# Loading each block of rows in sixteen groups of eight: which row goes to which partition, and what it does to the DMA engines

## The chip, the cores and the metric

The kernel runs on one core of a Trainium2 chip. The metric is the time of one execution in microseconds (us) of device time. Other words used here: PE is the matrix engine, PEld its weight loads, DVE the vector engine, ACT the scalar engine, POOL is GpSimd, SP the engine that issues the loads. Sixteen DMA engines move data from the memory (HBM) into SBUF, which has 128 partitions. A *load* is one DMA instruction; a *packet* is what one DMA engine moves at a time, here one row of a load (five loads of 128 rows of 16 KB left 640 packets of 16,384 bytes in the trace). A load *lands* when all sixteen engines have reported their share by a semaphore update (31 x 16 = 496 of these for the 31 loads of the kernel before). Engines are *in step* when they work on the same rows of their shares at the same time; a *lead* is how far one is ahead of another. *Partners* are two engines of which the author supposed that they hinder each other.

## The reference

For an array of 1024 x 8192 floats, the skewness of each row:

```python
def reference(x):
    mean = np.mean(x, axis=-1, keepdims=True)
    std = np.std(x, axis=-1, keepdims=True)
    z = (x - mean) / (std + 1e-8)
    return np.mean(z ** 3, axis=-1).astype(np.float32)
```

The 33.55 MB of input are read once. All the work is in reading them and in summing x, x squared and x cubed by row.

## The kernel before

Eight blocks of 128 rows, a row per partition. A block comes in 2 to 9 loads of some columns each; `UNITS` lists the widths. ACT squares with a running sum, DVE multiplies the square by x with a running sum, PE adds up transposed 128 x 128 pieces for the sum of x. The results stand as one column per block, are transposed at the end and stored.

```python
UNITS = [
    [512, 1024, 2560, 4096],
    [4096, 4096],
    # ... five blocks cut ...
    [1152, 1152, 1152, 1152, 1024, 896, 896, 512, 256],
]
X_BUFS = 8
# ...
    xv = x.rearrange("(b p) c -> b p c", p=P)
    ob = out.rearrange("(b p) -> b p", p=P)
# ...
    for b, widths in enumerate(UNITS):
        # ...
        for k, w in enumerate(widths):
            xt = xpool.tile([P, w], FP, tag="x", name=f"x_{b}_{k}")
            nc.sync.dma_start(out=xt, in_=xv[b, :, c0 : c0 + w])
            # ... squares on ACT, cubes on DVE, transposes on PE ...
# ...
    skT_ps = psum1.tile([NB, P], FP, tag="skT")
    nc.tensor.matmul(out=skT_ps, lhsT=skew, rhs=ident, start=True, stop=True, is_transpose=True)
```

Of the kernel before, what the change touches and what calls it, by code (L numbers as in the profile page):

```python
# [8 lines left out]
FP = mybir.dt.float32  # L9
# [21 lines left out]
def _slices(w):  # L31
    n = -(-w // SUB_MAX)
    step = -(-w // n // 128) * 128
    return [(s, min(s + step, w)) for s in range(0, w, step)]
# [3 lines left out]
def kernel(  # L38
# [5 lines left out]
    nc = tc.nc  # L44
    P = nc.NUM_PARTITIONS
# [5 lines left out]
    third = (1.0 / 3.0) ** 0.5  # L51
    assert len(UNITS) == NB and all(sum(u) == C for u in UNITS)

    xv = x.rearrange("(b p) c -> b p c", p=P)
    ob = out.rearrange("(b p) -> b p", p=P)


# [6 lines left out]
    onep = ctx.enter_context(tc.tile_pool(name="onep", bufs=1))  # L64
# [7 lines left out]
    nc.scalar.activation(out=tiny, in_=onesn, func=AF.Square)  # L72
    ident = onep.tile([P, P], FP, tag="ident")
    make_identity(nc, ident)
    s2u = onep.tile([P, L * MAXC], FP, tag="s2u")
    s3u = onep.tile([P, L * MAXC], FP, tag="s3u")
    nc.vector.memset(s2u, 0.0)
# [7 lines left out]
    skew = onep.tile([P, NB], FP, tag="skew")  # L85
# [4 lines left out]
    def small(name, n):  # L90
        return onep.tile([P, n], FP, tag=name, name=name)

    def finish_first_blocks():

        m2, m3 = small("m2a", L), small("m3a", L)
        for dst, src in ((m2, s2u), (m3, s3u)):
            nc.vector.tensor_reduce(  # L97
                out=dst, in_=src.rearrange("p (b c) -> p b c", c=MAXC), axis=X_AXIS, op=ALU.add
            )
        m1sq, m1sq3, nm1 = small("m1sqa", L), small("m1sq3a", L), small("nm1a", L)  # L100
        nc.scalar.activation(out=m1sq, in_=s1ps[:, 0:L], func=AF.Square)
        nc.scalar.activation(out=m1sq3, in_=s1ps[:, 0:L], func=AF.Square, scale=third)
        nc.scalar.activation(out=nm1, in_=s1ps[:, 0:L], func=AF.Copy, scale=-3.0)
        g = nc.gpsimd
        var, rr = small("vara", L), small("rra", L)
        g.tensor_tensor(out=var, in0=m2, in1=m1sq, op=ALU.subtract)  # L106
        g.tensor_tensor(out=m1sq3, in0=m1sq3, in1=var, op=ALU.add)  # L107
        g.tensor_tensor(out=m1sq3, in0=m1sq3, in1=nm1, op=ALU.mult)  # L108
        g.tensor_tensor(out=m3, in0=m3, in1=m1sq3, op=ALU.add)  # L109
        g.tensor_tensor(out=rr, in0=var, in1=expo, op=ALU.pow)  # L110
        g.tensor_tensor(out=skew[:, 0:L], in0=m3, in1=rr, op=ALU.mult)  # L111

    def close_block(b, tp):
        tsb = Tsb[b % 2]
        nc.scalar.copy(out=tsb, in_=tp)  # L115
        nc.tensor.matmul(out=s1ps[:, b : b + 1], lhsT=tsb, rhs=onesn, start=True, stop=True)  # L116

    for b, widths in enumerate(UNITS):
        last = b == L
        tp = psum.tile([P, P], FP, tag="tp", name=f"tp_{b}")  # L120
        c0 = 0
        j = 0
        for k, w in enumerate(widths):
            xt = xpool.tile([P, w], FP, tag="x", name=f"x_{b}_{k}")
            nc.sync.dma_start(out=xt, in_=xv[b, :, c0 : c0 + w])
            c0 += w
            for s, e in _slices(w):
                i = b * MAXC + j
                a2 = s2l[:, j : j + 1] if last else s2u[:, i : i + 1]
                a3 = s3l[:, j : j + 1] if last else s3u[:, i : i + 1]  # L130
                j += 1
                in_psum = last and k >= len(widths) - PSUM_SQ
                pool = psq if in_psum else sqpool
                sq = pool.tile([P, e - s], FP, tag="sq", name=f"sq_{b}_{k}_{s}")
                nc.scalar.activation(  # L135
                    out=sq, in_=xt[:, s:e], func=AF.Square, scale=s_scale, accum_out=a2
                )
                cube = cubes[:, 0 : e - s] if in_psum else sq
                nc.vector.scalar_tensor_tensor(  # L139
                    out=cube, in0=sq, scalar=1.0, in1=xt[:, s:e],  # L140
                    op0=ALU.mult, op1=ALU.mult, accum_out=a3,
                )
            n = w // P
            for c in range(n):
                nc.tensor.matmul(  # L145
                    out=tp, lhsT=xt[:, c * P : (c + 1) * P], rhs=ident,
                    start=(k == 0 and c == 0), stop=(c0 == C and c == n - 1),
                    is_transpose=True,
                )
        close_block(b, tp)  # L150
        if b == L - 1:
            finish_first_blocks()
# [14 lines left out]
        out=m3, in0=v3, scalar1=nm1, scalar2=m3, op0=ALU.mult, op1=ALU.add  # L167
# [1 line left out]
    nc.vector.tensor_tensor(out=skew[:, L:NB], in0=m3, in1=rr, op=ALU.mult)  # L169

    skT_ps = psum1.tile([NB, P], FP, tag="skT")
    nc.tensor.matmul(out=skT_ps, lhsT=skew, rhs=ident, start=True, stop=True, is_transpose=True)  # L172
    skT = small("skT", P)[0:NB, :]
    nc.vector.tensor_copy(out=skT, in_=skT_ps)  # L174
    nc.sync.dma_start(out=ob, in_=skT)
# [30 lines left out]
```

## Time and profile before

| | before |
|---|---|
| median time | 92.75 us in the 3 runs known when predicting; 92.5 us with the fourth |
| profiled span | 91.4 us |
| busy: DVE, ACT, PE | 73.9, 69.1, 68.0 us |
| DMA engines, 5 to 80 us | always busy (share 1.00 to 1.01), 413 to 430 GB/s |
| a packet of 16,384 bytes | 611 ns, at the 10th, 50th and 90th percentile |
| first packet, last landing of a load | 1.75 us, 84.9 us |

The lines are shown and read in the prediction. The packet times are computed from the trace's DMA records, which hold start, duration and size of each packet, though not the engine that moved it.

### The profile page before, as it was taken

What the parts mean: (1) busy time and instruction counts of PE and PEld (TensorE: products, weight loads), DVE (VectorE), ACT (ScalarE), POOL (GpSimd) and SP (SyncE); (2) the same over time, 40 slices, a digit from 0 to 9 for tenths busy, and PEclk for the clock granted to TensorE, in tenths of its full rate; (3) what the DMA queues carried; (4) which work ended last, traced back from release to release, by engine and by line L of the source; (5) the groups of instructions that cost most, each with busy time, mean ns of one, the idle gap of its engine ahead of it and who ended that gap; (6) DMA issues with size and microseconds to landing.
All of it is one profiled execution on the core that took longest, in us unless ns stands there. A gap on an engine that the chain in (4) does not pass through costs nothing. (4 is left out here: it accounts for less than half of the span.)

```text
span 91.4 us, 1437 instructions
## 1 busy us (share of the span) xinstructions
PE 68.0 (74%) x529; PEld 60.6 (66%) x529; DVE 73.9 (81%) x91; ACT 69.1 (76%) x101; POOL 9.4 (10%) x14
## 2 busy tenths in 40 slices
PE   0391898879495949688889897857789798989610
PEld 0360897779494939587879796747678687867500
DVE  0052290898989798978999999998899999999960
ACT  6350927969595959689889999766798899999830
POOL 3000000000000000000000000000000000699820
PEclk9999999999999999999999999999999999999995
DMA  1999999999999999999999999999999999991000
GB/s 43 362 374 440 445 438 409 430 452 430 402 423 452 442 417 434 435 424 399 430 414 404 430 420 420 423 407 422 419 409 423 406 418 408 406 344 74 0 0 2
DMA packets 4486, 33.64 MB, mean 368 GB/s; under 512 B 504, under 2 KB 640, under 8 KB 2560
## 3 DMA queue, kind: packets, MB, share of 16 engines
q1 hardware_dynamic: 4480, 33.56, 88.6%
q8 instruction: 4, 0.07, 0.3%
q14 instruction: 2, 0.02, 0.0%
HBM read 33.55 MB, written 0.00 MB: 367 GB/s over the span
## 5 line engine op out<-in xcount | busy, mean ns | idle before, releaser
L139 DVE SCALAR_TENSOR_TENSOR sq<-sq,x 128x2048 f32<-128x2048 f32 (+11 forms) x39 | 71.5, 1885 | 13.9 <-ACT sq L135 13.9
L145 PE MATMUL tp<-ident,x 128*128 128x128 f32 x512 | 65.2, 285 | 15.3 <-DMA x<-in_x_dram 15.0
L135 ACT ACTIVATE sq<-x 128x2048 f32<-128x2048 f32 (+12 forms) x41 | 62.8, 1534 | 17.4 <-DMA x<-in_x_dram 15.9
L145 PEld LDWEIGHTS tp<-ident,x 128*128 128x128 f32 x512 | 58.7, 147 | 20.5 <-DMA x<-in_x_dram 16.6
L106 POOL TENSOR_TENSOR vara<-m2a,m1sqa 128x7 f32<-128x7 f32 x1 | 1.3, 1294 | 77.1 <-DVE m3a L97 77.1
L135 ACT ACTIVATION_READ_ACCUMULATOR sq<-x 128x1 f32 x41 | 7.6, 186 | 0.0
L116 PEld LDWEIGHTS s1ps<-onesn,tsb 128*128 128x128 f32 x16 | 2.4, 188 | 5.6 <-ACT tsb L115 5.6
L116 PE MATMUL s1ps<-onesn,tsb 128*128 128x1 f32 x16 | 3.1, 260 | 3.7 <-ACT tsb L115 3.7
L139 DVE DVE_READ_ACCUMULATOR sq<-sq,x 128x1 f32 x39 | 3.2, 83 | 0.0
L110 POOL TENSOR_TENSOR rra<-vara,expo 128x7 f32<-128x7 f32 x1 | 2.6, 2624 | 0.0
L115 ACT COPY tsb<-tp 128x128 f32<-128x128 f32 x8 | 2.0, 249 | 0.0
L72 ACT ACT_TABLE_LOAD x1 | 1.3, 1283 | 0.7 <-PEq L190 0.7
L172 PE MATMUL skT_ps<-ident,skew 128*8 128x128 f32 x1 | 0.3, 273 | 2.0 <-DVE skew L169 2.0
L172 PEld LDWEIGHTS skT_ps<-ident,skew 128*8 128x8 f32 x1 | 0.1, 83 | 2.1 <-DVE skew L169 2.1
L107 POOL TENSOR_TENSOR m1sq3a<-m1sq3a,vara 128x7 f32<-128x7 f32 x1 | 1.2, 1202 | 0.1
L139 DVE SCALAR_TENSOR_TENSOR cubes<-sq,x 128x512 f32<-128x512 f32 (+1 forms) x2 | 1.1, 554 | 0.1
L108 POOL TENSOR_TENSOR m1sq3a<-m1sq3a,nm1a 128x7 f32<-128x7 f32 x1 | 1.1, 1150 | 0.0
L109 POOL TENSOR_TENSOR m3a<-m3a,m1sq3a 128x7 f32<-128x7 f32 x1 | 0.9, 935 | 0.1
L111 POOL TENSOR_TENSOR skew<-m3a,rra 128x7 f32<-128x7 f32 x1 | 0.9, 933 | 0.1
L70 DVE MEMSET onesn<- 128x1 f32 x1 | 0.1, 59 | 0.8 <-PEq L190 0.8
L163 POOL TENSOR_TENSOR rrl<-varl,expo 128x1 f32<-128x1 f32 x1 | 0.6, 562 | 0.6 <-ACT varl L161 0.6
L174 DVE COPY skT<-skT_ps 8x128 f32<-8x128 f32 x1 | 0.3, 278 | 0.4 <-PE skT_ps L172 0.4
(25 smaller groups left out, 4.4 us busy)
## 6 DMA issues: line engine op xcount, KB each, us to landing
x<-in_x_dram SPq DMA_DIRECT2D x5, 2048.0 KB, 18.7
x<-in_x_dram SPq DMA_DIRECT2D x5, 1024.0 KB, 24.2
x<-in_x_dram SPq DMA_DIRECT2D x4, 576.0 KB, 9.8
x<-in_x_dram SPq DMA_DIRECT2D x1, 2176.0 KB, 33.8
x<-in_x_dram SPq DMA_DIRECT2D x1, 1920.0 KB, 36.2
x<-in_x_dram SPq DMA_DIRECT2D x2, 896.0 KB, 15.8
x<-in_x_dram SPq DMA_DIRECT2D x1, 1664.0 KB, 33.9
x<-in_x_dram SPq DMA_DIRECT2D x1, 1408.0 KB, 30.3
```

The source lines that it names most:

```text
L72: nc.scalar.activation(out=tiny, in_=onesn, func=AF.Square)
L106: g.tensor_tensor(out=var, in0=m2, in1=m1sq, op=ALU.subtract)
L107: g.tensor_tensor(out=m1sq3, in0=m1sq3, in1=var, op=ALU.add)
L108: g.tensor_tensor(out=m1sq3, in0=m1sq3, in1=nm1, op=ALU.mult)
L109: g.tensor_tensor(out=m3, in0=m3, in1=m1sq3, op=ALU.add)
L110: g.tensor_tensor(out=rr, in0=var, in1=expo, op=ALU.pow)
L111: g.tensor_tensor(out=skew[:, 0:L], in0=m3, in1=rr, op=ALU.mult)
L115: nc.scalar.copy(out=tsb, in_=tp)
L116: nc.tensor.matmul(out=s1ps[:, b : b + 1], lhsT=tsb, rhs=onesn, start=True, stop=True)
L135: nc.scalar.activation(out=sq, in_=xt[:, s:e], func=AF.Square, scale=s_scale, accum_out=a2)
L139: nc.vector.scalar_tensor_tensor(out=cube, in0=sq, scalar=1.0, in1=xt[:, s:e], op0=ALU.mult, op1=ALU.mult, accum_out=a3,)
L145: nc.tensor.matmul(out=tp, lhsT=xt[:, c * P : (c + 1) * P], rhs=ident, start=(k == 0 and c == 0), stop=(c0 == C and c == n - 1), is_transp ...
```

## The change

The comment that came with it: "Within a block partition 8e+i takes row 16i+e, so that the sixteen DMA engines read neighbouring rows; the last transpose puts them back". The hope is a better reading order in the memory.

```diff
-    xv = x.rearrange("(b p) c -> b p c", p=P)
+    xv = x.rearrange("(b i e) c -> b e i c", e=16, i=8)
@@
+    unperm = onep.tile([P, P], FP, tag="unperm")
+    nc.gpsimd.tensor_copy(
+        out=unperm.rearrange("p (i e) -> p i e", e=16),
+        in_=ident.rearrange("p (e i) -> p i e", e=16),
+    )
@@
-            nc.sync.dma_start(out=xt, in_=xv[b, :, c0 : c0 + w])
+            nc.sync.dma_start(out=xt, in_=xv[b, :, :, c0 : c0 + w])
@@
-    nc.tensor.matmul(out=skT_ps, lhsT=skew, rhs=ident, start=True, stop=True, is_transpose=True)
+    nc.tensor.matmul(out=skT_ps, lhsT=skew, rhs=unperm, start=True, stop=True, is_transpose=True)
```

## The prediction

The forecast came to 92.75 + 75 x 0.5 = 130 us, from a worst case of 92.75 + 75 = 168 us. What is measured in it is the 92.75 us, the 75 us of full stream and the 611 ns; that a packet takes twice as long when partners are in step, and that half a load apart costs nothing, was supposition. Rival (c) is that partners hinder each other (theory P of the experiments).

> **What bounds the kernel now.** I read the busy shares first, then the strips over time, then the groups with their idle time, then the waits of the compute engines and of the load queue, and last the end of the run.
>
> ```profile
> PE 68.0 (74%) x529; PEld 60.6 (66%) x529; DVE 73.9 (81%) x91; ACT 69.1 (76%) x101; POOL 9.4 (10%) x14
> ...
> DVE  0052290898989798978999999998899999999960
> ...
> DMA  1999999999999999999999999999999999991000
> GB/s 43 362 374 440 445 438 409 430 452 430 402 423 452 442 417 434 435 424 399 430 414 404 430 420 420 423 407 422 419 409 423 406 418 408 406 344 74 0 0 2
> DMA packets 4486, 33.64 MB, mean 368 GB/s; under 512 B 504, under 2 KB 640, under 8 KB 2560
> ...
> q1 hardware_dynamic: 4480, 33.56, 88.6%
> ```
>
> No compute engine is full over the span of 91.4 us, but the DMA strip is: from the second slice (2.3 us each) to the thirty-sixth it stands at 9, and the rate is 400 to 450 GB/s throughout. So the sixteen DMA engines are the first suspect. The windows give the same in numbers:
>
> ```profile
> 5.00:20.00 15.00, 11.46 (x70) 10.34 (x71) 8.05 (x11) 8.62 (x12) 0.00 (x0) 1.00 1.01 426
> 20.00:40.00 20.00, 15.57 (x134) 14.46 (x133) 18.30 (x17) 15.86 (x19) 0.00 (x0) 1.00 1.01 430
> 40.00:60.00 20.00, 17.79 (x154) 16.52 (x153) 19.21 (x21) 18.55 (x23) 0.00 (x0) 1.00 1.00 419
> 60.00:80.00 20.00, 16.23 (x133) 14.10 (x132) 19.09 (x23) 16.88 (x26) 1.53 (x2) 1.00 1.01 413
> ```
>
> The columns are the stretch, its length, busy us of PE, PEld, DVE, ACT and POOL, the clock, the DMA share and GB/s. The DMA share is 1.00 in each stretch between 5 and 80 us, while DVE goes from 8.05 of 15 to 18.3 to 19.2 of 20. So the DMA engines are saturated and DVE is 4 to 8% behind them: two bounds, close together. The waits say who is first:
>
> ```profile
> ACT sq L135 <- DMA x<-in_x_dram: 15.9, 16, 3.1
> ...
> DVE sq L139 <- ACT sq L135: 13.9, 11, 3.5
> ```
>
> ACT waits for loads, DVE for ACT, nobody upstream waits for compute except the issue of loads, which waits 66.1 us in 23 waits for DVE to free one of the eight buffers (the queue's own waits). Since the engines still have packets at every moment, that wait costs nothing.
>
> The trace's packet records show what sort of limit this is. Each row of a load is one packet (31 loads x 128 rows = 3968; with one 4-byte semaphore packet per engine and load, 31 x 16 = 496, and 8 + 8 for the output, 4480). The 640 packets of 16,384 bytes took 611 ns at the 10th, at the 50th and at the 90th percentile: 16,384 / 611 = 26.8 GB/s per engine, 429 GB/s for sixteen. The 8192-byte ones took 312 ns at the median, 319 at the 90th. [...]Only the first loads are scattered (10,240 bytes: median 385, mean 418, longest 1332 ns).
>
> The end: the last load lands at about 85 us, DVE finishes its cubes at 87.8, the closing chain ends at 89.3 us, the store and the end of the program take the rest to 91.4. The measured median is 92.75 us, 1.35 above the profiled span.
>
> [...]
>
> **The change, part by part.**
>
> *Order of instructions.* Setting the two programs side by side, the order on every engine is the same; POOL has one instruction more, the loads have a source of three dimensions, the last transpose reads another constant.
>
> *The extra copy on POOL.* 128 x 128 elements after the identity, about 1.3 us into the run. The mask operation of the same size took 0.29 us, so I estimate 0.2 to 0.4 us. POOL is then idle until 78.4 us, the first load lands after 3.7 us and the copy is needed at 88.7. Cost on the path: 0.
>
> *The last transpose.* One matmul of the same shape, 0.27 us: 0.
>
> *Reading neighbouring rows: the intended gain.* The most it can bring is the scatter of the start. In the third load (2560 columns, 10,240 bytes a row) the mean packet is 33 ns over the median, times 8 packets per engine = 0.26 us; with the two loads before it, and the few outliers later, I estimate 0.5 to 1 us. Steady packets cannot get below 611 ns by a better row order if they already go at the engine's own pace. [...]So the gain is at most about 1 to 2 us, 1 to 2%, and DVE, 4 to 8% behind, would allow it.
>
> *Who writes where: the possible loss.* If the source's slowest dimension has 16 entries and each engine takes one, it writes partitions 8e to 8e+7, as the comment wants. [...]Worst case, in step: 16 KB packets take 2 x 611 = 1222 ns, the rate falls to 215 GB/s, and the 75 us of full stream become 150: 92.75 + 75 = 168 us. Best case, half a load apart: no loss. If the lead of one over the other lies anywhere between, the mean loss is half of that: 75 x 0.5 = 37.5 us, so 92.75 + 37.5 = 130 us. [...]DVE would catch up behind slow loads, so 1 to 2 us of the tail (85 to 87.8) would be hidden, less than I can resolve. I take 130 us.
>
> **The rivals.**
>
> (a) *Nothing moves* (92 to 94 us): [...]For it: engines drift apart by 1.6 to 3.0 us within a load (first to sixteenth semaphore update), so strict lockstep is not given. [...]I give 27%.
>
> (b) *The intended gain* (90.5 to 91.5 us): needs memory conflicts that the packet times do not show. Over 2% would need more than 1.9 us; 3%.
>
> (c) [...](115 to 165 us): 65%. A weak form, in which pairs fall out of step after the first loads (95 to 110 us), 5%.
>
> [...]
>
> **Range and chances.** (c) is the likeliest and its size is uncertain by its nature; (a) is the second peak. The central value is 130 us, the range 92.5 to 158 us, which spans both. Faster by over 2%: 0.03. Within 2%: 0.27. Slower by over 2%: 0.70.
>
> **What would show it.** Right: the rate strip at 215 to 330 GB/s with the DMA share still at 9 and 1.0; 16 KB packets at two values, near 611 and towards 1222 ns; the 10th percentile still 611 (each engine unhindered is as fast as before); DVE busy for the same 74 us but at 5 to 6 of 10 over the span; ACT's wait for loads up from 15.9 to some 50 us; the load queue waiting for the same buffers, which now come free right after landing. Wrong: packets still at 611 ns for all (then a), or below it (then b).[...]

## The result

The changed kernel took 163.0 us (median of 4 runs, 161.97 to 164.61) against 92.5 us (92.07 to 92.76). The ratio of the fast runs is 1.759, with a 95% interval of 1.746 to 1.773. A ratio here is the mean time of one kernel's fast runs over that of the other's in the same rounds, so it is not quite the ratio of the medians. The profiled run was the slowest of the four, 164.61 us, and counts as slow by the rule of 1.5% over the fastest; its clock (0.83) is that of the others (0.79 to 0.84), and nothing below rests on that difference.

The sign was right and the time was outside the range, which ended at 158 us. The page of the changed kernel: busy shares, strips, queue.

```profile
PE 92.0 (57%) x529; PEld 83.0 (51%) x529; DVE 75.4 (46%) x91; ACT 70.1 (43%) x101; POOL 5.8 (4%) x15
...
DVE  0215109146073280822909184445555544566573
...
DMA  4999999999999999998999999999999999999920
GB/s 122 232 225 193 258 193 193 225 225 193 193 246 205 193 197 239 227 194 189 227 207 202 222 216 215 209 223 225 219 224 224 227 227 226 236 238 237 253 60 1
...
q1 hardware_dynamic: 4480, 33.56, 95.1%
```

Its windows (columns as in the prediction: stretch, length, busy PE, PEld, DVE, ACT, POOL, clock, DMA share, GB/s):

```profile
5.00:20.00 15.00, 6.91 (x30) 5.71 (x29) 4.84 (x8) 3.77 (x7) 0.00 (x0) 1.00 1.01 214
20.00:40.00 20.00, 10.65 (x66) 10.09 (x66) 9.03 (x8) 8.06 (x9) 0.00 (x0) 0.91 1.01 212
40.00:60.00 20.00, 13.03 (x66) 12.71 (x66) 8.71 (x7) 8.06 (x9) 0.00 (x0) 0.66 1.03 215
60.00:80.00 20.00, 11.44 (x64) 10.88 (x63) 8.43 (x9) 8.27 (x9) 0.00 (x0) 0.75 1.02 213
```

The same 4480 packets and the same bytes, the DMA engines as busy as before, but half of the rate: 212 to 215 GB/s where before had 413 to 430. DVE and ACT did about the same work (75.4 and 70.1 us, before 73.9 and 69.1) and only waited longer. PE was busy for 92.0 us instead of 68.0 with the same 529 instructions, at a granted clock of 0.66 to 1.00 in these windows; it did not hold up the loads, for the DMA engines stayed at a share of 1.01 to 1.03. The waits of the engines:

```profile
DVE sq L145 <- ACT sq L141: 83.8, 29, 7.7
ACT sq L141 <- DMA x<-in_x_dram: 81.6, 29, 7.4
```

ACT's wait for loads went from 15.9 to 81.6 us. From the first packet to the last landing, the stream took 156.8 - 2.15 = 154.6 us against 84.9 - 1.75 = 83.2 before: 71.4 us more, and the profiled spans differ by 162.8 - 91.4 = 71.4. The whole loss is in the stream of loads.

What a packet looks like, from the DMA records (16,384 bytes, 640 packets in each kernel; ns):

```
before  10th / 50th / 90th percentile   611 /  611 /  611
after   10th / 50th / 90th percentile  1164 / 1272 / 1291
after, one load, a row of each of the sixteen engines at a time, medians of 16 packets:
  1168 1260 1282 1282 | 1176 1260 1284 1282   (from 21.3 us)
```

The packets start in groups of sixteen, within about 0.3 us of each other; a load is eight such groups. No packet kept its 611 ns (the shortest took 1133), and the durations repeat every four rows, not every eight.

The added copy on POOL, in the timeline (start, duration, instruction):

```profile
1.37 0.40 POOL L77 COPY unperm<-ident 128x128 f32<-128x128 f32 x1
```

It took 0.40 us at 1.37 us, 2.9 us before ACT began its first square and 158 us before it was needed.

### The profile page after: what moved, and what is told of

It reads as the page before. It is cut to its first block, busy times and chain, and to the rows that moved or that the text cites. A ratio compares the mean times of both kernels' runs of the same rounds, so it can differ in the third digit from the quotient of the medians.

```text
span 162.8 us, 1438 instructions
## 1 busy us (share of the span) xinstructions
PE 92.0 (57%) x529; PEld 83.0 (51%) x529; DVE 75.4 (46%) x91; ACT 70.1 (43%) x101; POOL 5.8 (4%) x15
## 3 DMA queue, kind: packets, MB, share of 16 engines
q1 hardware_dynamic: 4480, 33.56, 95.1%
## 4 chain that ended last, share of the span: by engine, by line
DMA 58%; PE 15%; another core or an unknown queue 11%; ACT 8%; DVE 3%; SPq 2%; issue 1%; ACTq 0%; DVEq 0%
DMA x<-in_x_dram 58%; PE tp L151 14%; ACT sq L141 7%; DVE sq L145 2%; SPq L131 2%; PE s1ps L122 0%; ACT tsb L121 0%; DVE cubes L145 0%; PE skT_ps L178 0%; DVE m3l L172 0%; DVE skT L180 0%; ACT m1sql L166 0%; DVE m3l L163 0%; DVE skew L175 0%
## 5 line engine op out<-in xcount | busy, mean ns | idle before, releaser
L151 PE MATMUL tp<-ident,x 128*128 128x128 f32 x512 | 88.7, 348 | 63.4 <-DMA x<-in_x_dram 63.4
L151 PEld LDWEIGHTS tp<-ident,x 128*128 128x128 f32 x512 | 80.5, 184 | 70.3 <-DMA x<-in_x_dram 66.0
L145 DVE SCALAR_TENSOR_TENSOR sq<-sq,x 128x2048 f32<-128x2048 f32 (+11 forms) x39 | 72.8, 1887 | 83.8 <-ACT sq L141 83.8
L141 ACT ACTIVATE sq<-x 128x2048 f32<-128x2048 f32 (+12 forms) x41 | 62.8, 1531 | 81.6 <-DMA x<-in_x_dram 81.6
L116 POOL TENSOR_TENSOR rra<-vara,expo 128x7 f32<-128x7 f32 x1 | 1.5, 1519 | 0.0
```

The source lines that it names most:

```text
L116: g.tensor_tensor(out=rr, in0=var, in1=expo, op=ALU.pow)
L141: nc.scalar.activation(out=sq, in_=xt[:, s:e], func=AF.Square, scale=s_scale, accum_out=a2)
L145: nc.vector.scalar_tensor_tensor(out=cube, in0=sq, scalar=1.0, in1=xt[:, s:e], op0=ALU.mult, op1=ALU.mult, accum_out=a3,)
L151: nc.tensor.matmul(out=tp, lhsT=xt[:, c * P : (c + 1) * P], rhs=ident, start=(k == 0 and c == 0), stop=(c0 == C and c == n - 1), is_transp ...
```

## The experiments

Theories: **P**, DMA engines that are in step hinder each other in pairs, because each now writes eight neighbouring partitions. It is a supposition: the records name neither an engine nor the partition that a packet goes to, so no trace shows the pairs, or what partners would meet at. **M**, sixteen neighbouring rows read at once collide in the memory. **D**, the three-dimensional source is costly for the DMA engines. The results were correct in all runs. The profiled runs of four kernels below (half of the partitions, the lead of a half and no lead within the queue, the quarter with a third extra load) are 6.2, 2.8, 3.8 and 3.8% over their fastest; what is read from them are differences of a fifth and more.

### Neighbouring rows, but in groups of four

```diff
-    xv = x.rearrange("(b i e) c -> b e i c", e=16, i=8)
+    xv = x.rearrange("(b i e) c -> b e i c", e=32, i=4)
```

(and the same 32 in the copy that makes `unperm`)

> Loads again with a three-dimensional source and with neighbouring rows read at once, but in 32 groups of 4 rows (partition 4e+i takes row 32i+e) instead of 16 groups of 8; the constant for the last transpose is made to match. Theory P[...]: [...]16 KB packets are back at 611 ns, the rate at 420 GB/s, the time within 1% of before, 92 to 93.5 us. Theory M (sixteen neighbouring rows collide in the memory): as slow as the changed kernel, 155 to 165 us. Theory D (the three-dimensional source itself costs the DMA engines): as slow as the changed kernel too.

Measured: 93.72 us (93.45 to 94.03) against 93.06 us, ratio 1.009 (1.005 to 1.013). M and D fall: by the source pattern the rows read at once are again neighbours, the source has again three dimensions, and the packets are at 611 ns. Its windows:

```profile
5.00:20.00 15.00, 10.75 (x62) 9.63 (x62) 6.96 (x11) 7.91 (x11) 0.00 (x0) 1.00 1.00 409
20.00:40.00 20.00, 15.62 (x133) 14.50 (x132) 18.41 (x17) 15.91 (x18) 0.00 (x0) 1.00 1.01 431
40.00:60.00 20.00, 17.51 (x148) 16.14 (x148) 19.21 (x19) 18.10 (x22) 0.00 (x0) 1.00 1.00 419
60.00:80.00 20.00, 16.61 (x134) 14.48 (x134) 19.23 (x23) 17.25 (x25) 0.72 (x1) 1.00 1.01 414
```

From 20 us on the rates are 431, 419 and 414 where before had 430, 419 and 413. So the intended gain, a better reading order, is nil in the steady stream. The 0.9% is lost before 20 us: the rate there is 409 against 426, which over 15 us is about 0.6 us of stream, and the first packet starts at 2.13 instead of 1.75 us. The median issue of a load took 535 ns on SP, against 328 ns before. That the longer issue makes the slow start was not tested by itself.

### Groups of eight, but no neighbouring rows

```diff
-    xv = x.rearrange("(b p) c -> b p c", p=P)
+    xv = x.rearrange("(B e h i) c -> B h e i c", e=16, h=2, i=8)
@@
-            nc.sync.dma_start(out=xt, in_=xv[b, :, c0 : c0 + w])
+            nc.sync.dma_start(out=xt, in_=xv[b // 2, b % 2, :, :, c0 : c0 + w])
```

(made from the kernel before, with four stores that put the results in their places)

> 16 groups of 8 as in the change[...], but no neighbouring rows at once: each group is eight consecutive rows, groups 16 rows apart (a tile takes half of the rows of two blocks; four small stores put the result in order, some 1 to 2 us). Theory P: 16 KB packets towards 1250 ns, rate near 215 GB/s, 160 to 166 us. Theory M: no neighbouring rows, so about 93 to 95 us. Theory D: slow, as the change.

Measured: 154.06 us (152.03 to 161.09), ratio 1.643 (1.630 to 1.657). Slow without neighbouring rows, so M falls a second time. It was 6 us faster than P had said. The windows show where:

```profile
20.00:40.00 20.00, 11.13 (x66) 10.57 (x66) 9.02 (x8) 8.06 (x9) 0.00 (x0) 0.76 1.01 219
60.00:80.00 20.00, 13.03 (x68) 12.47 (x68) 9.29 (x8) 8.27 (x9) 0.00 (x0) 0.66 1.00 218
120.00:140.00 20.00, 15.59 (x104) 13.33 (x104) 15.13 (x20) 13.66 (x23) 4.39 (x5) 0.87 1.01 307
```

The rate is 219 GB/s for the long rows and rises to 307 towards the end. The half rate is thus no fixed cap of such loads. This run does not say why it rises; it made me suspect that the state of the engines to each other matters.

### Half of the partitions in a load, and its control with half of the columns

Both from the kernel before, with the natural row order and two-dimensional sources:

```diff
-            nc.sync.dma_start(out=xt, in_=xv[b, :, c0 : c0 + w])
+            for h in (0, 64):                                   # half of the partitions
+                nc.sync.dma_start(out=xt[h : h + 64, :], in_=xv[b, h : h + 64, c0 : c0 + w])
```

```diff
-            nc.sync.dma_start(out=xt, in_=xv[b, :, c0 : c0 + w])
+            for h in (0, w // 2):                               # control: half of the columns
+                nc.sync.dma_start(out=xt[:, h : h + w // 2], in_=xv[b, :, c0 + h : c0 + h + w // 2])
```

> The kernel before with each load cut in two, partitions 0 to 63 and 64 to 127, natural row order, two-dimensional source. [...]Theory P: [...]packets near twice as long, 155 to 168 us. Theories M and D: no neighbouring rows at once beyond what before has, no third dimension, so 93 to 98 us, the price of twice as many loads.

> Control for the run with half of the partitions: each load cut in two by columns, so as many loads and as many packets of half the size, but 128 partitions each. All theories: 93 to 98 us (3968 more packets at 9 ns over 16 engines are 2.2 us, some of it hidden). If this one is slow as well, the number of loads[...] made the other slow.

(The 9 ns for a packet: in the trace of before, packets of 2048 and 10,240 bytes took 84 and 385 ns at the median, and the line through the two leaves 9 ns at no bytes.)

Measured: 160.01 us (151.75 to 161.58; the runs scatter and three of the four count as slow beside the fastest, so no ratio is given) and 95.46 us (95.08 to 96.8, ratio 1.026). Their windows from 20 to 40 us, the half partitions first:

```profile
20.00:40.00 20.00, 13.35 (x66) 12.85 (x66) 9.03 (x8) 8.06 (x9) 0.00 (x0) 0.66 1.00 212
```

```profile
20.00:40.00 20.00, 15.42 (x128) 13.77 (x128) 17.43 (x15) 15.72 (x17) 0.00 (x0) 1.00 1.01 421
```

The rates are 212 and 421 GB/s. So loads that use none of the change's row order, and none of its source shape, are as slow as the change (212 to 215 GB/s) when each writes 64 partitions. Twice as many loads cost under 3 us (95.46 against 93.06 us).

### Loads of one size: the base lines, and a lead for half of the engines

To test whether partners can get out of each other's way, all loads were given 2048 columns, 8192-byte rows, first in the kernel before and in the changed kernel:

```diff
+UNITS = [[2048] * 4 for _ in range(8)]
+PSUM_SQ = 0
```

> The kernel before with all loads of 2048 columns (8192-byte rows, 32 loads of 1 MiB) and the squares of the last block in SBUF. It is the base line of the next three, which need loads of one size. Expected 95 to 99 us: the same stream, a later first landing and a longer last piece (2048 columns instead of 256 to finish after the last landing). Packets 312 ns.

> The changed kernel with all loads of 2048 columns. Theory P, engines in step: packets 600 to 640 ns, 160 to 170 us.

Measured: 93.96 us (93.94 to 94.2) and 164.61 us (163.66 to 165.53). The first is 1 us under the 95 to 99 that were expected, the second within its 160 to 170. In the second one the sixteen semaphore updates of the first seven loads all came within 520 to 540 ns, in a load that takes 4.7 us, and the offsets stayed the same from load to load. From the eighth load on (40 us) one engine came 1.3 us after the others and stayed there; the other fifteen were still within 0.52 us at 59 us. In this run the engines go in step (0.52 to 0.54 us in a load of 4.7 us), and the one lead (1.3 us) is kept over many loads.

The next two put extra loads that nothing reads in front, to set some engines back. The larger ones have rows of 32 KB, half of an engine's share of a load (4 of its 8 rows of 8 KB), and by the design they leave every engine half a load behind or ahead of its partner; with a quarter the rows have 16 KB:

```diff
+    nc.sync.dma_start(out=lag1[0:96:8, :], in_=x[0:12, 0:8192])    # 0:4096 for a quarter
+    nc.sync.dma_start(out=lag2[0:16:4, :], in_=x[0:4, 0:8192])
     for b, widths in enumerate(UNITS):
```

> The same as the uniform changed kernel, with two extra loads in front that nothing reads: one of 12 rows of 32 KB[...], and one of 4 rows[...].[...] Theory P with leads that last: packets back to 309 to 330 ns after the start, and the time at the uniform base line plus about 4 us (the extra bytes), 99 to 104 us, with the loads otherwise unchanged. Theory P with leads that get lost: starts fast, falls back to 215 GB/s. Theories M and D: nothing changes but 2 to 4 us more, 165 to 173 us.

> As the run with a lead of half a load, with extra rows of 16 KB, a quarter of an engine's share. Theory P with leads that last: [...]four rows take 1.5 times as long, some packets stay at 309 ns and some go to 620, the rate is near 285 GB/s, and the time near 97 + 39 + 2 = 138 us (130 to 145). If leads get lost: as the uniform changed kernel.

Measured: 162.13 us (160.77 to 164.97) and 164.88 us (163.24 to 165.49). P had said 99 to 104 and 130 to 145: both missed. The extra loads show twelve and four updates with their data, so twelve and then four engines took them; that these are the ones which set partners apart, on which the design rests, no trace shows. The landings tell that the leads had not been made. With the quarter all sixteen updates of a load came within 0.52 us, as without it: the extra loads were over before the first real one had arrived. With the half, four engines were 2.4 us ahead (about half of a load's 4.6 us) and the other twelve within 0.6 us of each other. So the test was badly built, but the second outcome was odd: four engines half a load ahead, by the design out of the way of their partners, and yet no packet between 30 and 80 us took less than 450 ns.

### The same leads, made within the queue

```diff
             xt = xpool.tile([P, w], FP, tag="x", name=f"x_{b}_{k}")
+            if b == 0 and k == 3:
+                nc.sync.dma_start(out=lag1[0:96:8, :], in_=x[0:12, 0:8192])   # 0:4096 for a quarter
+                nc.sync.dma_start(out=lag2[0:32:8, :], in_=x[0:4, 0:8192])
             nc.sync.dma_start(out=xt, in_=xv[b, :, :, c0 : c0 + w])
```

The control without a lead has `lag1[0:128:8, :]` and `lag2[0:128:8, :]` from `x[0:16, 0:8192]`.

> The first lead runs did not make the lead they were meant to make: the extra loads were over, or nearly, when the first real load arrived[...]. Here the two extra loads (12 rows and 4 rows of 32 KB) stand in the queue behind three real loads, so that engines already have work waiting and the lead in bytes is exact[...]. Theory P with leads that last: about 16 us at 222 GB/s and the extra rows, then packets of 309 to 330 ns and 400 GB/s and more: 100 to 110 us.[...]

> The same with extra rows of 16 KB, a lead of a quarter of a load's share. Theory P: [...]4 rows take 1.5 times 1.24 us = 1.85 us instead of 2.3 to 2.4, the rate is 285 to 310 GB/s, the time 130 to 143 us.[...]

> Control: the two extra loads at the same place, but of 16 rows[...], so that no engine gets ahead of another. All theories: the uniform changed kernel (164.6 us) plus 1 MiB more bytes at 222 GB/s, 4.7 us: 167 to 171 us. If this is fast, the extra loads did something other than shift the engines.

Measured: with a lead of half a load 117.57 us (114.81 to 119.86; three of the four count as slow beside the fastest, so no ratio), with a quarter 160.42 us (158.15 to 163.53, ratio 1.730), without a lead 170.43 us (163.16 to 171.93). The windows of the run with half a load:

```profile
10.00:15.00 5.00, 3.86 (x25) 3.22 (x23) 2.47 (x3) 2.21 (x4) 0.00 (x0) 1.00 0.99 220
25.00:30.00 5.00, 5.00 (x28) 5.00 (x28) 2.79 (x3) 3.95 (x5) 0.00 (x0) 0.59 1.01 397
30.00:40.00 10.00, 8.75 (x74) 7.78 (x72) 8.71 (x8) 8.10 (x9) 0.00 (x0) 1.00 1.01 381
80.00:90.00 10.00, 6.25 (x52) 5.46 (x51) 7.47 (x7) 6.25 (x8) 0.00 (x0) 1.00 1.02 318
```

and of the run with a quarter, in the same stretches after the extra loads:

```profile
25.00:30.00 5.00, 4.22 (x26) 3.82 (x25) 2.30 (x2) 2.49 (x3) 0.00 (x0) 0.65 1.04 241
30.00:40.00 10.00, 5.42 (x41) 4.86 (x40) 4.80 (x5) 5.03 (x7) 0.00 (x0) 0.94 1.01 233
```

The rate jumps from 220 to 397 GB/s at the two extra loads, with the loads themselves unchanged. The control, with extra loads at the same place but no lead, stays at 218 to 227 GB/s between 30 and 120 us. So it is not a fixed cost of such loads: the same rows, from the same places, by the same instructions, come at 220 GB/s before the leads and at 397 after them. That fits P; that it is partners which are then apart is not shown. In the first loads after the extra ones the updates come in groups of four, eight and four engines, 1.2 to 1.4 us apart, as the lags want it; which engines these are, the records do not name. The time missed its 100 to 110 us as the order wears off: the landings of a load spread from 2.7 us early to 7 us, and the rate falls to 318 at 80 to 90 us. By my estimate the start cost about 10 us, the lower rate about another 10 (29.5 MB at a mean of some 365 instead of 420 GB/s), and 94 + 20 is within 4 us of the measured time.

The quarter missed in the other direction. By P, partners should then hinder each other for half of their bytes, at 285 GB/s by the estimate of the expectations (two rows at 309 ns, two at 600); it was 233 to 247.

### Why a quarter was worth nothing

By the design the two extra loads of 12 and 4 rows set four engines back by 32 KB, eight by 16 KB and four by nothing. The author supposed that then some pairs hinder each other just while the others do not. If a hindered pair slows all sixteen engines (theory K), the loads are slow all the time; if each pair goes for itself (theory N), they are not. Two runs test it. A third extra load, of 8 rows, makes the lags 48, 32, 16 and 0 KB, by the supposition with all pairs hindered at the same times. Or the first extra load stays alone, by the supposition with eight engines always free of their partners and eight always in step.

```diff
                 nc.sync.dma_start(out=lag1[0:96:8, :], in_=x[0:12, 0:4096])
                 nc.sync.dma_start(out=lag2[0:32:8, :], in_=x[0:4, 0:4096])
+                nc.sync.dma_start(out=lag3[0:64:8, :], in_=x[0:8, 0:4096])    # quarter, a third load
```

```diff
                 nc.sync.dma_start(out=lag1[0:96:8, :], in_=x[0:12, 0:8192])
-                nc.sync.dma_start(out=lag2[0:32:8, :], in_=x[0:4, 0:8192])    # first load alone
```

> The quarter lead gave 238 GB/s (160 us), not the 285 of the step that the prediction rested on. [...]This run adds an extra load of 8 rows of 16 KB[...]. Theory K: [...]four rows take about 1.24 + ... = (2 x 309 + 2 x 600) ns = 1.8 us, rate near 285 GB/s, time 130 to 142 us, packets of 309 and of 600 side by side. Theory N (each pair for itself, and a part lead is worth little for another reason): unchanged, 157 to 163 us.

> Only the extra load of 12 rows of 32 KB[...]. Theory K: all packets[...] stay at 490 to 640 ns, 222 to 240 GB/s, and no packets of 309 ns after the start, 160 to 168 us. Theory N: [...]about half of the packets are near 309 ns and the DMA share falls to 0.75; the time is about the same.

Measured: 143.85 us (142.07 to 147.44, ratio 1.538) and 163.95 us (162.44 to 165.98, ratio 1.761). Windows of the first, then of the second:

```profile
10.00:15.00 5.00, 3.99 (x19) 3.59 (x19) 2.38 (x3) 2.21 (x4) 0.00 (x0) 1.00 1.01 221
25.00:30.00 5.00, 4.54 (x28) 4.31 (x29) 2.30 (x2) 3.20 (x3) 0.00 (x0) 0.73 1.01 285
```

```profile
10.00:15.00 5.00, 4.04 (x20) 3.64 (x19) 2.33 (x3) 2.31 (x4) 0.00 (x0) 1.00 1.04 229
25.00:30.00 5.00, 4.10 (x19) 3.70 (x20) 2.30 (x2) 2.37 (x3) 0.00 (x0) 0.50 1.04 233
30.00:40.00 10.00, 6.70 (x46) 6.38 (x45) 4.60 (x4) 5.00 (x6) 0.00 (x0) 0.81 1.00 224
```

With the third load, the same quarter lead gives the 285 GB/s at first (it wears off to 255 to 285, which is why the time ended 2 us over the expected 130 to 142). With the first extra load alone all stay at 224 to 235 GB/s, the DMA share stays at 0.99 to 1.05, and not one packet is fast. The packets of 8192 bytes that started between 30 and 80 us, from the DMA records:

```
run (us)                          packets  under 330 ns  median ns  10th to 90th
before, loads of one size  (94)     2562      2558          312       309 to 320
after, loads of one size  (165)     1355         0          614       512 to 638
lead of a half            (118)     2257      1067          335       314 to 413
lead of a quarter         (160)     1440         0          560       482 to 618
quarter, a third load     (144)     1667       111          512       341 to 602
first extra load alone    (164)     1389         0          601       494 to 621
no lead, same extra loads (170)     1351         0          614       521 to 634
```

These runs speak against N, which had put about half of the packets near 309 ns and the DMA share at 0.75 with the first extra load alone: 0 of 1389 packets were under 330 ns, at a share of 0.99 to 1.05. N had also put the run with the third load at 157 to 163 us, and it took 143.85. The runs fit K, and no more than that: which engines are partners is supposed, and how one slow pair would slow the others is not visible in a trace and was not tested by a run.

### The copy and the last transpose alone

```diff
-    xv = x.rearrange("(b i e) c -> b e i c", e=16, i=8)
+    xv = x.rearrange("(b p) c -> b p c", p=P)
@@
-        in_=ident.rearrange("p (e i) -> p i e", e=16),
+        in_=ident.rearrange("p (i e) -> p i e", e=16),
```

(against the changed kernel; the index of the load goes back to that of before with it)

> The extra copy on GpSimd and the last transpose through its result, with the loads of before (the copy keeps the order). All theories: 0.4 us on an idle engine, off every path: 92 to 93.5 us, within 0.5% of before. If it were at fault for a part of the 0.9% by which the run with groups of four was slower, it would be 93.5 or more; I expect that part to be the longer issue of a three-dimensional load (537 ns against 328 ns) at the start.

Measured: 92.69 us against 92.95 us, ratio 1.001 (0.994 to 1.009). They cost nothing.

## Why the prediction was right and wrong

**Right: the bound and the size of the hope.** The DMA engines were the bound (share 1.00 to 1.01 from 5 to 80 us), and a better row order had little to give: the run with groups of four shows neighbouring rows at an unchanged 431, 419 and 414 GB/s and packets at the same 611 ns. The hoped-for gain was nil. One reading was too smooth: the rate strip was not at 400 to 450 GB/s throughout, it has 362 and 374 in its second and third slices and 344 in the thirty-sixth. Nothing rests on that.

**Right: where the loss comes from.** The DMA engines stay busy (share 0.98 to 1.03 between 5 and 140 us) with packets twice as long (1272 ns at the median against 611), and rival (c), 115 to 165 us, held the time. The runs with groups of four (93.72 us), with half of the partitions (160.01 us) and with a half-load lead (117.57 us) show from three sides that it is which partitions are grouped in a load, and how the engines stand to each other, and not the row order or the source's shape. That each engine has eight neighbouring partitions, and that the engines hinder each other in pairs, remains supposed, for the records do not name engines; the effect of the leads fits it.

**Right: the small parts.** The copy cost 0.40 us on an idle engine (estimated 0.2 to 0.4), the last transpose nothing, DVE was busy for 75.4 us (said: the same 74).

**Wrong: the step "If the lead of one over the other lies anywhere between, the mean loss is half of that".** It made 130 us out of a worst case of 168 us and moved the whole range down, so that it ended at 158 us, below the worst case that the same paragraph had worked out. Two things were mistaken in it. First, leads are not spread evenly. In the changed kernel the first and the last engine finish the first two 2 MiB loads of 16 KB rows within 0.23 and 0.21 us, in a load that takes 10 us. Of the drift of 1.6 to 3.0 us that rival (a) took from the kernel before, some 1.5 us comes later, but in single engines: one lags by 1.5 us from 42 us on, two from 82 us, and at 101 us fourteen of the sixteen are still within 0.2 us. The engines also hardly ever ran out of packets (DMA share 0.98 to 1.03 between 5 and 140 us): they started together, and most stayed so. Second, a part lead did not help by its share. The quarter lead gave 233 to 247 GB/s, and only with the third extra load the 285 of the estimate. So the loss is not the mean over independent pairs. In place of the term 75 x 0.5 = 37.5 us, the runs show the full term: 71.4 us more stream, against 75 in the worst case.

**Wrong: some of the signs.** The 10th percentile of the 16 KB packets was to stay at 611 ns; it was 1164. Nor did the packets take two values: all lay between 1133 and 1402 ns, so in this run no packet went unhindered. They were uniformly longer, twice as long at the median (1272 against 611 ns), and the packet times alone did not tell the memory from the partitions; it took the experiments to tell. ACT's wait grew to 81.6 us instead of some 50, for the same reason.

**The chances** were 0.70 for slower, which came, and 0.65 for (c).

## What to carry to other kernels

When a load's source pattern is reshaped, look at how its outer dimension groups the partitions: with 128 partitions as the outer dimension on both sides, or 32 outer groups, a core read at 413 to 431 GB/s from 20 us on, with 16 outer groups of eight at 212 to 220 in the long loads, from the same bytes. Look at the packet times first: here packets of one size took 611 ns almost without exception, and a new row order left them at 611 ns. A range should hold the worst case that one can work out, unless a measurement speaks against it.
